# Down projections of two feed-forward blocks: sixteen of 22 chunks by seven products of quarters

## The chip, the cores and the metric

The kernel runs on one core of a Trainium2 chip. The metric is the device time of one execution in microseconds (us); the time before is 3135.24 us, the median of three runs (3134.79 to 3135.58). PE is TensorE's matmul row of the profile, PEld its weight loads, DVE is VectorE, ACT is ScalarE, POOL is GpSimd, SP is the engine whose queue issues nearly all DMAs.

## The reference, cut to what matters

Three blocks of a network run one after the other on 1024 tokens of width 1024. The first and the third end in a feed-forward part whose hidden width is D_FF = 2816, which is 22 chunks of 128. The change is in the last product of both, the down projection:

```
up = causal_depthwise_conv(h @ w_up[l], conv_w[l], conv_b[l])      # block 1
a, bgate = jnp.split(up, [D_FF], axis=-1)
x = x + (jax.nn.silu(a) * bgate) @ w_down[l]
```

Block 3 is the same without the conv, with x scaled by ALPHA, and with another norm behind it. All data are float32.

## The kernel before, in words

**Precision.** A float32 product is made of three matmuls. Each operand is split into hi, a copy in the reduced type F32R, and lo, the difference of the operand and hi. A product of 128 x 128 weights and 128 x 512 values is hi·hi + hi·lo + lo·hi (mm, line 345). split (line 349) makes hi on ScalarE and lo by a subtraction on GpSimd or VectorE.

**Layout.** Everything is transposed: features lie on partitions, tokens in two halves of 512 columns. X[j][half] holds feature block j (0 to 7) of the residual stream in SBUF. The gated hidden activations of chunk c and token half are written to DRAM (gd, g_out, line 173) and read back as G[c, half] (g_dma, line 1361). All weights stand in one DRAM array, wall, as tiles of 128 x 1024 in the order of their use, and SP loads them into raw.

**The up projections** (strassen, line 1256) already use seven products of quarters in place of eight. s_steps (line 1203) makes the weights' side of it out of two raw tiles ra and rb in six steps: A22, S1 and S3 are 512 wide, A1 and S24 are 1024 wide. Each is a cast on ScalarE and a subtraction on GpSimd, and four more GpSimd subtractions or additions form the sums. Raw tiles alternate between two pools (s_dma, line 1247).

**The down projections** (down, line 1423) take two chunks at a time: for each of 8 feature blocks and 2 halves one PSUM bank gets six matmuls, and VectorE adds it to X[j][half]. So each pair of chunks has 16 groups of six matmuls and 16 adds. Nine such pairs (18 chunks) are followed by the last four chunks, which are summed in PSUM over all four before a single add, since norms and outputs hang on them. Beside a pair, the next pair's G tiles are split: half 0 on GpSimd, half 1 on VectorE (g_split, line 1365). Weight tiles come through w_load (line 369), which keeps four of them split ahead; w_retire loads the next.

**Order.** The order of the program is fixed by hand: every engine carries out its instructions strictly in the order in which the Python code emits them, and waits at the head of its queue when an operand or a buffer is not there. self.bank gives PSUM banks from a pool of six, and pools hand out released buffers in the order of their release. The tag h has 64 buffers of 128 x 512 in SBUF. tail (line 1381) is called during the last round of the up projection: it starts the first weights, the first G tiles and the 16 X tiles (x_load, line 1376). In block 1 self.left then holds four pieces of the last chunk's conv, which down emits after its adds 0, 3, 6 and 9; in block 3 it holds one gate. Work of other generators (Driver, line 191) is not due in these stretches.

Of the kernel before, what the change touches and what calls it, by code (L numbers as in the profile page):

```python
# [9 lines left out]
F32 = mybir.dt.float32  # L10
# [29 lines left out]
def _weights(a):  # L40
# [9 lines left out]
    def ffn(up, down):  # L50
        ab = _chunks_a(a[up][0])
        dn = a[down][0].reshape(NFF, 128, D)
        out = []

        def u(c):
            out.extend([ab[c], ab[NFF + c]])

        for c in range(NFF):
            u(c)
        out.extend(dn[:NFF - 4])  # L60
        for j in range(4):
            out.append(np.concatenate([dn[k][:, 256 * j:256 * j + 256] for k in range(NFF - 4, NFF)], axis=1))
        return out

    t = []
# [32 lines left out]

S_TILES = ((38, 38), (178, 180))

# [198 lines left out]
class Kernel:  # L299
# [947 lines left out]
    def s_dma(self, n):  # L1247

        pool = self.up if (n + self.lead) % 2 else self.wp
        for _ in range(2):  # L1250
            raw = pool.tile([128, 1024], F32, tag="raw", bufs=2, name="raw")
            self.nc.sync.dma_start(out=raw, in_=self.a["wall"][self.wd])
            self.wd += 1
            self.sraws.append(raw)
# [77 lines left out]
    def ffn(self, evac, put, later, add_last, done, by_half, alpha=None, lead=2):  # L1332
# [5 lines left out]
        with ExitStack() as ctx:  # L1338
# [32 lines left out]

            def g_group(i):
                cs = (2 * i, 2 * i + 1) if i < NFF // 2 - 2 else range(NFF - 4, NFF)
                return [(c, half, i % 2 and c < NFF - 1) for c in cs for half in range(2)]

# [5 lines left out]
            def tail(n):  # L1381
# [6 lines left out]
                elif n == 1:  # L1388
                    for a in g_group(0):
                        g_dma(*a[:2])  # L1390
                    for j in range(2):
                        x_load(j)
                elif n == 2:
                    for j in range(2, 5):
                        x_load(j)
                else:
                    for a in g_group(0):
                        g_split(*a, nc.gpsimd)
                    for j in range(5, 8):
                        x_load(j)  # L1400
                    for a in g_group(1):
                        g_dma(*a[:2])

# [18 lines left out]

            def down(i, ws):
                n = 0
                loads = g_group(i + 1)
                gap = 12 // len(loads)
                for j in range(8):
                    for half in range(2):
                        ps = self.bank("dn")
                        for k in range(2):  # L1430
                            whi, wlo = ws[k]
                            ghi, glo = G[2 * i + k, half]
                            c = slice(128 * j, 128 * j + 128)
# [4 lines left out]
                        x = X[j][half]  # L1438
                        if alpha and i == 0:
                            self.stt(x, x, alpha, ps, ALU.mult, ALU.add)  # L1440
                        else:
                            self.tt(x, ps, x, ALU.add)
                        n += 1
                        if n % 3 == 1 and self.left:
                            self.left.pop(0)()
                        if n % gap == 0 and loads and n > 2:
                            g_split(*loads.pop(0))

            for i in range(NFF // 2 - 2):
                ws = self.w_take(2)  # L1450
                if i == 0:
                    self.w_retire(0)
                yield from down(i, ws)
                if i < NFF // 2 - 3:
                    for a in g_group(i + 2):
                        g_dma(*a[:2])
                self.w_retire(2)
            full, q0, q1 = slice(0, HF), slice(0, HF // 2), slice(HF // 2, HF)
# [1008 lines left out]
```

## Time and profile before

| | |
|---|---|
| median of the runs | 3135.24 us |
| profiled execution | 3131.53 us |
| span of the profiled execution | 3129.7 us |
| PE busy | 2941.2 us (94%) |
| DVE busy | 1803.3 us (58%) |
| POOL busy | 1432.9 us (46%) |
| ACT busy | 1284.8 us (41%) |
| mean granted clock | 0.964 |

The span is the time from the first to the last instruction. Matmuls are pipelined, so the duration of a single one (0.39 us) is longer than the distance to the next. Instructions of VectorE also overlap a little: the next one starts before the end shown for the one before. A row of the form "dn<-ghi,whi" names what is written and what is read; a wait stands in square brackets with what ended it. In the first block the down projection runs from about 904 to 1145 us, in the third from about 2851 to 3103.

### The profile page before, as it was taken

Reading aid. Unit: us, or ns where it says so; the run is one execution under the profiler, and the core shown is the slowest. Engines: PE = TensorE matmul, PEld = TensorE weight load, DVE = VectorE, ACT = ScalarE, POOL = GpSimd, SP = SyncE. Lnnn points to the kernel's source line nnn. Section 1 sums busy time; section 2 is a strip of 40 time slices with the busy share of each in tenths; the row PEclk is TensorE's granted clock in tenths of the full one; section 3 lists DMA queues with packets and bytes.
Section 4 is the critical chain, followed back from the end, with each engine's and each line's share of the span. In section 5 each row is a group of like instructions: output and inputs, shape, how many; then the busy total and the mean of one; then the engine's idle time right before and its main releaser. Section 6 shows DMA issues by size and latency. Waiting matters only on the chain. (4 is left out here: it accounts for less than half of the span.)

```text
span 3129.7 us, 41397 instructions
## 1 busy us (share of the span) xinstructions
PE 2941.2 (94%) x15188; PEld 2499.6 (80%) x15188; DVE 1803.3 (58%) x3522; ACT 1284.8 (41%) x2493; POOL 1432.9 (46%) x1008
## 2 busy tenths in 40 slices
PE   8999998999999999889998989989899899999997
PEld 6898776888878877868897778977678688888886
DVE  6444246666665569966645665577667522224556
ACT  4232224444432153556673356654444422222223
POOL 4313434777743365862214342144333477774330
PEclk9999999999999999999998989999889999999998
DMA  4101241222252312131113232110222222225321
GB/s 159 33 23 51 72 134 41 81 81 81 81 188 82 108 49 80 40 109 50 44 39 118 84 121 64 42 32 27 68 68 98 84 81 81 86 79 179 108 81 54
DMA packets 114876, 248.96 MB, mean 80 GB/s; under 512 B 19696, under 2 KB 31600, under 8 KB 114672
## 3 DMA queue, kind: packets, MB, share of 16 engines
q1 hardware_dynamic: 114384, 246.01, 24.0%
q8 instruction: 120, 1.97, 0.3%
q14 instruction: 84, 0.69, 0.1%
q10 hardware_dynamic: 288, 0.30, 0.0%
HBM read 192.52 MB, written 53.74 MB: 79 GB/s over the span
## 5 line engine op out<-in xcount | busy, mean ns | idle before, releaser
L332 POOL TENSOR_TENSOR wlo<-raw,whi 128x1024 fp32r<-128x1024 f32 x240 | 582.2, 2436 | 862.0 <-ACT whi L326 846.5
L326 ACT ACTIVATE whi<-raw 128x1024 fp32r<-128x1024 f32 x240 | 248.3, 1053 | 537.0 <-PE dn L347 283.2
L332 DVE TENSOR_TENSOR X<-dn,X 128x512 f32<-128x512 f32 (+1 forms) x312 | 209.9, 676 | 161.7 <-PE dn L347 159.5
L347 PE MATMUL dn<-ghi,whi 128*128 128x512 f32 (+1 forms) x736 | 281.1, 382 | 0.6 <-DVE X L332 0.6
L347 PE MATMUL dn<-glo,whi 128*128 128x512 f32 (+1 forms) x736 | 280.2, 381 | 0.0
L347 PE MATMUL dn<-ghi,wlo 128*128 128x512 f32 (+1 forms) x736 | 280.2, 381 | 0.0
L332 POOL TENSOR_TENSOR raw<-raw 128x512 f32<-128x512 f32 x156 | 203.0, 1302 | 12.1
L332 POOL TENSOR_TENSOR slo<-raw,shi 128x512 fp32r<-128x512 f32 x117 | 150.7, 1302 | 106.2 <-ACT shi L326 104.9
L347 PE MATMUL p<-thi,shi 128*128 128x512 f32 x468 | 185.1, 395 | 13.9 <-DVE u L1105 9.8
L332 DVE TENSOR_TENSOR v<-p,e 128x512 f32<-128x512 f32 x78 | 53.8, 690 | 243.8 <-ACT e L326 194.3
L347 PE MATMUL p<-tlo,shi 128*128 128x512 f32 x468 | 183.9, 393 | 0.0
L347 PE MATMUL p<-hhi,wlo 128*128 128x512 f32 x468 | 182.2, 389 | 1.7 <-POOL wlo L332 1.7
L347 PE MATMUL p<-thi,slo 128*128 128x512 f32 x468 | 183.7, 393 | 0.0
L347 PE MATMUL p<-hhi,whi 128*128 128x512 f32 x468 | 182.1, 389 | 0.0
L347 PE MATMUL p<-hlo,whi 128*128 128x512 f32 x468 | 182.1, 389 | 0.0
L329 DVE SCALAR_TENSOR_TENSOR t<-u,vec,t 128x512 f32<-128x512 f32 x176 | 132.9, 755 | 79.5 <-ACT t L326 74.2
L347 PE MATMUL qk<-hhi,whi 128*128 128x512 f32 x384 | 162.2, 422 | 7.8 <-ACT hhi L326 7.2
L332 POOL TENSOR_TENSOR beta<-beta,f 128x511 f32<-128x511 f32 (+3 forms) x96 | 91.2, 956 | 154.0 <-DVE beta L336 137.8
L347 PEld LDWEIGHTS dn<-ghi,whi 128*128 128x128 f32 x736 | 139.2, 189 | 27.6 <-DVE X L332 1.3
L347 PEld LDWEIGHTS dn<-ghi,wlo 128*128 128x128 f32 x736 | 139.1, 189 | 26.4
L347 PEld LDWEIGHTS dn<-glo,whi 128*128 128x128 f32 x736 | 139.2, 189 | 26.0
L347 PE MATMUL op<-hhi,wlo 128*128 128x512 f32 x384 | 153.2, 399 | 4.0 <-POOL wlo L332 4.0
(400 smaller groups left out, 8150.7 us busy)
## 6 DMA issues: line engine op xcount, KB each, us to landing
raw<-in_wall SPq DMA_DIRECT2D x240, 512.0 KB, 3.8
gd<-g SPq DMA_DIRECT2D x88, 256.0 KB, 2.2
gx<-gd SPq DMA_DIRECT2D x88, 256.0 KB, 5.2
x2d<-X SPq DMA_DIRECT2D x64, 256.0 KB, 2.0
X<-x2d SPq DMA_DIRECT2D x64, 256.0 KB, 5.3
x<-in_xT SPq DMA_DIRECT2D x16, 256.0 KB, 6.0
X<-in_xT SPq DMA_DIRECT2D x16, 256.0 KB, 4.6
T<-in_rpbx SPq DMA_DIRECT2D x8, 448.0 KB, 3.6
```

What stands on the lines that cost most here:

```text
L326: self.nc.scalar.activation(out=out, in_=in_, func=func, bias=bias, scale=scale, **kw)
L329: self.nc.vector.scalar_tensor_tensor(out=out, in0=in0, scalar=s, in1=in1, op0=op0, op1=op1)
L332: (eng or self.nc.vector).tensor_tensor(out=out, in0=in0, in1=in1, op=op)
L347: self.nc.tensor.matmul(out=out, lhsT=lhsT, rhs=rhs, start=start, stop=stop, skip_group_check=more)
```

## The change

In both blocks chunks 0 and 1 stay as they were (first_down). Chunks 2 to 17 become four quads of four chunks. Within a quad, the weights are a 2 x 2 arrangement of quarters (feature blocks 0 to 3 or 4 to 7, by the first or last two chunks of the quad), and so are the activations (first or last two chunks, by token half). Each quad is done in two sets, s = 0 and 1, of two feature blocks out of the upper and two out of the lower half. A set has seven products of two feature blocks each, so 14 groups of six matmuls; I number them 0 to 13, in the order of plan in seven(). There are no sums in SBUF of the products: a bank is accumulated further after it was read, and each state of it that belongs to some part of X is added there by VectorE, 14 adds a set. An even set is one with s = 0, an odd one has s = 1.

The weights' side comes out of s_steps as in the up projection, a set ahead. The activations' side, b_steps, is made on ScalarE and VectorE once per quad, for the next quad: products 1, 2 and 3 take G tiles as they are (two casts and two subtractions, "lows"), products 5, 6, 7 and 4 first form differences (two subtractions, two casts, two lows each). The differences of products 5, 6 and 4 are written to PSUM (t), those of product 7 over G in SBUF. todo says after which add of a set each step is emitted. The last four chunks are done as before; their splits are emitted during the last quad, and the weight loads through w_load stop in between (S_TILES). The conv pieces of block 1 are emitted after adds 0 to 3.

```diff
@@ -57,7 +57,10 @@
 
         for c in range(NFF):
             u(c)
-        out.extend(dn[:NFF - 4])
+        out.extend(dn[:2])
+        for i in range(2, NFF - 4, 4):
+            for col in (0, 512, 256, 768):
+                out.append(np.concatenate([dn[k][:, col:col + 256] for k in range(i, i + 4)], axis=1))
...
@@ -96,7 +99,7 @@

-S_TILES = ((38, 38), (178, 180))
+S_TILES = ((38, 38), (78, 78), (178, 180), (220, 220))
...
@@ -1246,7 +1249,9 @@
 
     def s_dma(self, n):
-        pool = self.up if (n + self.lead) % 2 else self.wp
+        self.s_raws(self.up if (n + self.lead) % 2 else self.wp)
+
+    def s_raws(self, pool):
         for _ in range(2):
             raw = pool.tile([128, 1024], F32, tag="raw", bufs=2, name="raw")
             self.nc.sync.dma_start(out=raw, in_=self.a["wall"][self.wd])
@@ -1369,9 +1374,13 @@
...
-            def g_group(i):
-                cs = (2 * i, 2 * i + 1) if i < NFF // 2 - 2 else range(NFF - 4, NFF)
-                return [(c, half, i % 2 and c < NFF - 1) for c in cs for half in range(2)]
+            def g_raw(cs):
+                for c in cs:
+                    for half in range(2):
+                        g_dma(c, half)
+
+            head, quads = (0, 1), [range(i, i + 4) for i in range(2, NFF - 4, 4)]
+            ends = range(NFF - 4, NFF)
 
...
@@ -1386,20 +1395,21 @@
                     self.w_load()
                     self.w_load()
                 elif n == 1:
-                    for a in g_group(0):
-                        g_dma(*a[:2])
+                    g_raw(head)
                     for j in range(2):
                         x_load(j)
+                    self.s_raws(self.up)
                 elif n == 2:
                     for j in range(2, 5):
                         x_load(j)
                 else:
-                    for a in g_group(0):
-                        g_split(*a, nc.gpsimd)
+                    for c in head:
+                        for half in range(2):
+                            g_split(c, half, False, nc.gpsimd)
                     for j in range(5, 8):
                         x_load(j)
-                    for a in g_group(1):
-                        g_dma(*a[:2])
+                    g_raw(quads[0])
+                    self.s_raws(self.wp)
 
...
-            def down(i, ws):
+            def b_steps(cs, B):
+
+                t = [None, None]
+
+                def pair(n, k, src):
+                    hi, lo = self.h("ghi", F32R), self.h("glo", F32R)
+                    B.setdefault(n, ([], []))
+                    B[n][0].append(hi)
+                    B[n][1].append(lo)
+                    self.act(hi, src, AF.Copy)
+                    return lo, src, hi
+
+                def raw(n, o, half):
+                    for low in [pair(n, k, G[cs[o + k], half]) for k in range(2)]:
+                        self.tt(*low, ALU.subtract)
+
+                def made(n, outs, parts):
+                    lows = []
+                    for k in range(2):
+                        p, q = parts(k)
+                        self.tt(outs(k), p, q, ALU.subtract)
+                        lows.append(pair(n, k, outs(k)))
+                    for low in lows:
+                        self.tt(*low, ALU.subtract)
+
+                def t1():
+                    for k in range(2):
+                        t[k] = self.pt.tile([128, 512], F32, tag="t", name="t")
+                    made(5, lambda k: t[k], lambda k: (G[cs[k], 1], G[cs[k], 0]))
+
+                return [lambda: raw(1, 0, 0), t1,
+                        lambda: made(6, lambda k: t[k], lambda k: (G[cs[2 + k], 1], t[k])),
+                        lambda: raw(2, 2, 0),
+                        lambda: made(7, lambda k: G[cs[k], 1], lambda k: (G[cs[2 + k], 1], G[cs[k], 1])),
+                        lambda: raw(3, 2, 1),
+                        lambda: made(4, lambda k: t[k], lambda k: (G[cs[2 + k], 0], t[k]))]
+
+            def first_down(ws, todo):
                 n = 0
-                loads = g_group(i + 1)
-                gap = 12 // len(loads)
                 for j in range(8):
                     for half in range(2):
                         ps = self.bank("dn")
                         for k in range(2):
                             whi, wlo = ws[k]
-                            ghi, glo = G[2 * i + k, half]
+                            ghi, glo = G[k, half]
                             c = slice(128 * j, 128 * j + 128)
                             self.mm(ps, whi[:, c], ghi, k == 0, False)
                             self.mm(ps, whi[:, c], glo, False, False)
                             self.mm(ps, wlo[:, c], ghi, False, k == 1)
                         yield 6 * 216.0
                         x = X[j][half]
-                        if alpha and i == 0:
+                        if alpha:
                             self.stt(x, x, alpha, ps, ALU.mult, ALU.add)
                         else:
                             self.tt(x, ps, x, ALU.add)
+                        if self.left:
+                            self.left.pop(0)()
+                        for f in todo.get(n, ()):
+                            f()
                         n += 1
-                        if n % 3 == 1 and self.left:
-                            self.left.pop(0)()
-                        if n % gap == 0 and loads and n > 2:
-                            g_split(*loads.pop(0))
-
-            for i in range(NFF // 2 - 2):
-                ws = self.w_take(2)
-                if i == 0:
-                    self.w_retire(0)
-                yield from down(i, ws)
-                if i < NFF // 2 - 3:
-                    for a in g_group(i + 2):
-                        g_dma(*a[:2])
-                self.w_retire(2)
+
+            def seven(s, A, B, todo):
+
+                banks, n = {}, 0
+                plan = ((1, "c", "A1", 0, 0, 0), (5, "f", "S1", 0, 4, 1), (6, "c", "S24", 0, 0, 1),
+                        (2, "d", "A1", 512, 0, 0), (7, "c", "S3", 0, 4, 1), (3, "f", "S24", 512, 0, 1),
+                        (4, "c", "A22", 0, 4, 0))
+                for p, key, w, off, row, half in plan:
+                    for m in range(2):
+                        start = (key, m) not in banks
+                        if start:
+                            banks[key, m] = self.bank("dn")
+                        ps = banks[key, m]
+                        whi, wlo = A[w]
+                        for k in range(2):
+                            c = slice(off + 256 * k + 128 * m, off + 256 * k + 128 * m + 128)
+                            hi, lo = B[p][0][k], B[p][1][k]
+                            self.mm(ps, whi[:, c], hi, start and k == 0, False, not start)
+                            self.mm(ps, whi[:, c], lo, False, False, not start)
+                            self.mm(ps, wlo[:, c], hi, False, k == 1, not start)
+                        yield 6 * 216.0
+                        x = X[row + 2 * s + m][half]
+                        self.tt(x, ps, x, ALU.add)
+                        for f in todo.get(n, ()):
+                            f()
+                        n += 1
+
+            A, B = {}, {}
+            ss, bs = self.s_steps(0, A), b_steps(quads[0], B)
+            todo = {2 * i: [f] for i, f in enumerate(ss)}
+            for n, f in zip((5, 7, 9, 11, 13, 15), bs):
+                todo.setdefault(n, []).append(f)
+            ws = self.w_take(2)
+            yield from first_down(ws, todo)
+            self.w_retire(2)
+            over = bs[6:]
+            n_sets = 2 * len(quads)
+            for n in range(n_sets):
+                i, s = n // 2, n % 2
+                todo = {1: over} if n == 0 else {}
+
+                def at(x, f):
+                    todo.setdefault(x, []).append(f)
+
+                nxt = {}
+                if n + 2 < n_sets:
+                    self.s_raws(self.wp if n % 2 else self.up)
+                if n + 1 < n_sets:
+                    for x, f in zip((0, 1, 2, 5, 7, 10), self.s_steps(n + 1, nxt)):
+                        at(x, f)
+                if s == 0:
+                    nb, cs = {}, quads[i + 1] if i + 1 < len(quads) else ends
+                    at(2, lambda cs=cs: g_raw(cs))
+                    if i + 1 < len(quads):
+                        bs = b_steps(cs, nb)
+                        for x, f in zip((8, 10, 12), bs):
+                            at(x, f)
+                    else:
+                        for x, c in zip((6, 8, 10, 12), cs):
+                            at(x, lambda c=c: g_split(c, 0, False))
+                elif i + 1 < len(quads):
+                    for x, f in zip((3, 5, 7, 9), bs[3:]):
+                        at(x, f)
+                else:
+                    def more():
+                        del self.stops[0]
+                        self.wi += 2 * n_sets
+                        self.w_load()
+                        self.w_load()
+
+                    at(0, more)
+                    for x, c in zip((3, 5, 7, 9), ends):
+                        at(x, lambda c=c: g_split(c, 1, c < NFF - 1))
+                yield from seven(s, A, B, todo)
+                A = nxt
+                if s:
+                    B = nb
+            self.w_retire(0)
...
```

## Rows read from the trace of the kernel before

**Rows 1.** The page, busy time, share of the span and instructions

```profile
PE 2941.2 (94%) x15188; PEld 2499.6 (80%) x15188; DVE 1803.3 (58%) x3522; ACT 1284.8 (41%) x2493; POOL 1432.9 (46%) x1008
```

**Rows 2.** Stretches of the span, with their columns, both projections

```profile
core 0: us, PE busy (x) PEld busy (x) DVE busy (x) ACT busy (x) POOL busy (x), PEclk, DMA share, GB/s
560.00:880.00 320.00, 320.00 (x1414) 265.05 (x1412) 202.88 (x354) 147.53 (x218) 229.49 (x150) 1.00 0.24 80
926.00:948.00 22.00, 22.00 (x98) 18.00 (x97) 15.36 (x24) 4.60 (x7) 7.80 (x4) 1.00 0.47 156
2850.00:3050.00 200.00, 200.00 (x885) 165.58 (x884) 113.42 (x167) 42.19 (x62) 73.62 (x42) 1.00 0.37 123
```

**Rows 3.** Instructions in order of time (start, us), around one slot

```profile
1000.27 0.39 PE L347 MATMUL dn<-ghi,whi 128*128 128x512 f32 x1
1000.47 0.69 DVE L332 TENSOR_TENSOR X<-dn,X 128x512 f32<-128x512 f32 x1 [0.67 <-PE dn L347]
1001.07 0.68 DVE L332 TENSOR_TENSOR glo<-gx,ghi 128x512 fp32r<-128x512 f32 x1
1001.63 0.39 PE L347 MATMUL dn<-ghi,whi 128*128 128x512 f32 x1
```

**Rows 4.** Groups by line and shape: count, busy us, mean ns, idle before

```profile
L332 POOL TENSOR_TENSOR wlo<-raw,whi 128x1024 fp32r<-128x1024 f32 x240 | 582.2, 2436 | 862.0 <-ACT whi L326 846.5 <-issue 15.1 <-DVE ql L329 0.5
L332 DVE TENSOR_TENSOR X<-dn,X 128x512 f32<-128x512 f32 x296 | 203.3, 690 | 161.1 <-PE dn L347 158.9
L332 POOL TENSOR_TENSOR raw<-raw 128x512 f32<-128x512 f32 x156 | 203.0, 1302 | 12.1
L332 DVE TENSOR_TENSOR glo<-gx,ghi 128x512 fp32r<-128x512 f32 x40 | 28.3, 708 | 3.7 <-ACT ghi L326 3.7
```

**Rows 5.** In order of time, ScalarE and GpSimd before the first projection

```profile
887.44 1.06 ACT L326 ACTIVATE whi<-raw 128x1024 fp32r<-128x1024 f32 x1 [9.28 <-DMA raw<-in_wall]
888.58 4.72 POOL L332 TENSOR_TENSOR wlo<-raw,whi 128x1024 fp32r<-128x1024 f32 x2 [9.87 <-ACT whi L326]
899.37 2.19 ACT L326 ACTIVATE ghi<-gx 128x512 fp32r<-128x512 f32 x4
```

**Rows 6.** In order of time, VectorE and GpSimd around 520

```profile
519.33 2.40 POOL L332 TENSOR_TENSOR wlo<-raw,whi 128x1024 fp32r<-128x1024 f32 x1 [13.66 <-ACT whi L326]
520.56 3.42 DVE L332 TENSOR_TENSOR X<-X 128x512 f32<-128x512 f32 x2
521.80 3.32 POOL L332 TENSOR_TENSOR raw<-raw 128x512 f32<-128x512 f32 x2
526.29 2.39 POOL L332 TENSOR_TENSOR wlo<-raw,whi 128x1024 fp32r<-128x1024 f32 x1 [1.17 <-ACT whi L326]
527.74 1.49 DVE L332 TENSOR_TENSOR tlo<-X,thi 128x512 fp32r<-128x512 f32 x1 [3.76 <-ACT thi L326]
```

**Rows 7.** Groups by line and shape, block 2's convolution

```profile
L329 DVE SCALAR_TENSOR_TENSOR cd<-u,vec,cd 128x512 f32<-128x512 f32 x133 | 100.2, 754 | 3.6
L332 POOL TENSOR_TENSOR cp<-cp,cm 128x512 f32<-128x512 f32 x70 | 91.3, 1307 | 34.5 <-ACT cm L326 30.3
```

**Rows 8.** In order of time, VectorE on a piece of conv

```profile
919.48 1.55 DVE L329 SCALAR_TENSOR_TENSOR t<-u,vec,t 128x512 f32<-128x512 f32 x2
921.06 0.69 DVE L332 TENSOR_TENSOR g<-t,a 128x512 f32<-128x512 f32 x1
```

**Rows 9.** The stretch in which the last projection begins

```profile
2850.00:2870.00 20.00, 20.00 (x90) 16.55 (x89) 11.48 (x18) 5.35 (x8) 10.04 (x7) 1.00 1.02 385
```

**Rows 10.** Stretches after the first projection, and TensorE's wait in them

```profile
1150.00:1155.00 5.00, 2.28 (x14) 2.20 (x14) 3.56 (x4) 4.49 (x7) 3.78 (x3) 0.85 0.00 2
1155.00:1160.00 5.00, 5.00 (x14) 4.03 (x15) 2.96 (x4) 3.34 (x5) 5.00 (x4) 0.50 0.18 29
1160.00:1165.00 5.00, 5.00 (x31) 4.36 (x30) 3.11 (x15) 0.21 (x2) 1.29 (x5) 0.96 0.21 80
1152.54 1.05 PE L347 MATMUL st<-ones,s 128*128 128x1 f32 x8 [3.87 <-POOL s L332]
```

## The prediction

> **What bounds the kernel now.** I read the page's busy shares first, then cut the span into stretches around the two down projections, then opened one product group, and last looked at each engine's queue around it. On the page TensorE is busy 94% of the span [rows 1]. In the stretches it is busy for all 22.00 us of 926 to 948 and for all 200.00 us of 2850 to 3050, at full clock, while VectorE works 113, GpSimd 74 and ScalarE 42 of those 200 us [rows 2]: the down projections are TensorE's alone. One group of six matmuls takes 1000.27 to 1001.63, so 1.36 us, 0.2267 us a matmul [rows 3]. I call such a group a slot. VectorE's add of a slot into X begins 0.20 us after the slot, and an instruction queued behind it starts 0.60 us later [rows 3], though the add itself lasts 0.69 [rows 4].
>
> **The change, part by part.**
>
> *Matmuls.* Sixteen chunks cost 8 pairs x 16 slots = 128 slots per block now, and 8 sets x 14 = 112 afterwards. 16 slots x 1.36 = 21.8 us go per block, 43.5 us in all, as long as nothing else keeps TensorE waiting.
>
> *Work on the other engines.* X adds fall from 128 to 112 per block. Per quad of chunks (two sets, 38.1 us of TensorE) VectorE gets 28 adds and 22 subtractions: 50 x 0.605 = 30.3 us. GpSimd gets per set seven 512-wide and two 1024-wide subtractions: at 1.27 and 2.38 us apart [rows 4, 5] 13.7 us, so 27.3 per quad; the up projections already run it 229 of 320 us beside a fully busy TensorE [rows 2]. ScalarE has 14 + 6 casts at about 0.56 and 4 at 1.0 [rows 5], 15 us. By busy time alone everything fits, and the full 43.5 us would be won. What decides is how the queues hold one another.
>
> *How late an add may be.* Banks are handed out in the order of their release, so a new set does not wait for the last adds of the old one. But plan's key "c" accumulates products 1, 6, 7 and 4 in the same two banks with an add between each: slot 4 needs add 0, slot 8 add 4, slot 12 add 8, with three slots (4.08 us) between. VectorE may thus lag about 3.1 us. In the kernel before no add sat behind more than one or two other instructions, and a bank came up again only after five further slots.
>
> *The port.* At 519.33 GpSimd starts a 2.40 us subtraction; VectorE's X<-X pair begins at 520.56 and takes 3.42 us instead of about 1.3 (0.605 and 0.69). Read through: the first of the pair gets on only when GpSimd's ends at 521.73, GpSimd's next (two in 3.32 instead of 2 x 1.30 [rows 4]) then goes, and the second waits for it. At 527.74 a tlo takes 1.49 instead of 0.69: it ends 0.55 after GpSimd's instruction [rows 6]. So VectorE and GpSimd alternate, one instruction each; a delayed VectorE instruction costs 0.47 after the other has ended, and GpSimd gets on about 0.45 after that starts. Where one VectorE operand is in PSUM there is nothing of it: the conv's 133 steps on cd average 754 ns, beside GpSimd's 70 at 1307 [rows 7]. The new subtractions with both inputs in SBUF are the lows of products 1, 2 and 3, the differences of product 5 and all four of product 7: 12 of 22 per quad, beside a GpSimd that is busy 72% of the time.
>
> The Trainium skill (SBUF — State Buffer, Who interferes with whom) says that a VectorE instruction with two SBUF inputs contends with a GpSimd instruction that reads SBUF, and that whoever starts first holds the pair for the whole instruction; it speaks against this change. The rows agree on the exclusion, but GpSimd gets on after 0.45 us of a 0.69 us instruction; with the whole time between instructions held, the walk below loses 6 to 7 us more.
>
> *One quad, step by step* (us from the start of an even set; casts and lows reach the next engine 0.08 after their shown end, as wlo at 888.58 follows the cast that ended at 888.50 [rows 5]). GpSimd's last subtraction of the set before ends at 3.2, its next five end at 4.4, 5.7, 7.0, 8.3, 9.5, then the 1024-wide one at 11.9. Adds 0 to 8 are on time, add 8 until 13.05. Product 1's lows: 13.2 to 13.6, then GpSimd until 14.9, then until 15.4. Adds 9 and 10 until 16.6. Product 5's differences meet GpSimd's S24 subtraction (16.1 to 18.5); that product is through at 21.1, adds 11 and 12 at 22.3, product 6 at 24.95, add 13 at 25.55. The set's matmuls ended at 19.04. Odd set: add 0 ends at 26.2, slot 4 was due at 24.48 and starts at 26.3: **1.84 lost**. ScalarE was held by product 6's casts until 24.2, so GpSimd's new round starts at 24.9 and its S3 subtraction ends only at 31.25; product 2's casts stand behind S3's cast (29.4), the first low waits for cast and port until 31.25, the second for the 1024-wide one until 34.1. Add 4, ready at 27.9, ends at 35.2; slot 8 was due at 31.77 and starts at 35.3: **3.56 lost**. Product 7 runs 35.8 to 39.5, adds 6 and 7, product 3 until 41.9, add 8 until 42.5; slot 12, due at 40.77, starts at 42.7: **1.94 lost**. Product 4 follows and the next even set starts with VectorE 0.4 us behind, as at first. A quad so takes 45.4 us; the same four chunks now take 32 slots, 43.5.
>
> *Whole down projection.* Quads 1 and 2 lose 7.34 each. Quad 3 has no next quad to prepare: 0. Quad 0 loses 12.0, since 18 of its own subtractions begin in first_down's slot 5 and VectorE enters set 0 behind (add 0 is through 9 us late, slot 4 starts 5.7 late). Block 3: 26.7 us. Block 1 has also four conv pieces, now in first_down's slots 0 to 3 rather than 0, 3, 6 and 9, each some 1.5 us of steps and up to 0.69 for the gate [rows 8]; first_down's VectorE work is then about 16 x 0.605 + 18 x 0.605 + 9 = 30 us against 21.8 of slots, which costs 7 more beyond what six banks cushion: 33.6. Together 60.3 lost against 43.5 won: **16.8 us slower**.
>
> *Other edits.* The tail's burst carries 1 MB more before first_down (8 G loads instead of 4; the weight loads are as many as before) at a time when the DMA engines are full (385 GB/s [rows 9]): at most 3 us per block; G is needed from slot 5 on and the second pair of raws a phase later, so I take 0. On SP's queue block 1's two gd writes now stand behind 10 issues instead of 4; they are read in set 6. The half-0 splits of the last chunks move 5 us of GpSimd work to set 6, when nothing on VectorE contends.
>
> *Clock.* A wait of 3.87 us was followed by granted 0.85, 0.50 and 0.96 in three 5 us stretches (0.50 is the 1.2 GHz level) [rows 10]: 3.4 us of matmul time. Eight waits here come near or beyond that. Since the next wait behind each would take up what is lost, I take 0, and up to 1.5 for each of the six 3.56 us waits and 3.4 for each of the two 5.7 us ones, 16 us, as the upper end.
>
> *Sum.* The profiled execution took 3131.53 us (span 3129.7 and 1.8 around it); with 16.8 more it is 3148.3. The median of the runs is 3.7 above that execution: **3152 us**.
>
> **The rivals.** *The port hardly decides (faster).* If VectorE's subtractions fall mostly into GpSimd's gaps, the same walk without port waits loses 2.3 us in block 3 (quad 0: 0.6; 0.9 at set 1's slot 12; 0.4 in quads 1 and 2 each) and 9.2 in block 1 (first_down 3.1, set 0 4.5, the rest 1.6): 3135.2 - 43.5 + 11.5 = 3103 us. For it: glo<-gx,ghi now averages 708 ns on VectorE, nearly undelayed [rows 4]. Against it: GpSimd is then busy 37% [rows 2], not 72%. *Half of the port waits.* The order of two queues turns on tenths of a us: if the 1024-wide subtraction does not cut in (2.4 us of the 3.56), and the differences of product 5 miss S24's, a quad loses 3 to 4, quad 0 7, block 1 some 6 more: about 38 to 40 lost, 3131 us. It is here that the sign turns. *Clock and burst on top.* All the upper ends at once: 3152 + 16 + 6 = 3174; against it, slow matmuls give VectorE time to catch up.
>
> **How the numbers follow.** Forecast 0.53, its own range 3139 to 3166 (one 1024-wide wait more or less per quad, 6 x 2.4 us); hardly any port loss 0.24, 3100 to 3125; half 0.15, 3126 to 3139; clock and burst 0.08. Runs within 0.2% (6.3 us) of 3135 count as the same. Faster: 0.24 + 0.05 of the half case and 0.01 of the forecast, 0.30. Same: 0.09 of the half case and 0.06 of the forecast, 0.15. Slower: 0.55. The range reaches from inside the first rival to inside the last: 3106 to 3169.
>
> **What would show it.** Right: TensorE in 948 to 1060 and 2890 to 3010 is no longer full, with waits for VectorE's X adds at slots 4, 8 and 12 of odd sets, 1.5 to 4 us each; low and difference subtractions on VectorE average over 0.9 us with single ones over 2; the last quad runs without waits. Wrong: some 174 us per block up to the last four chunks (196 now) with TensorE full, subtractions near 0.69 us, or waits on weights (S24, A1) or on B operands in place of the adds.

## The result, and the profile after

The changed kernel took 3151.28 us (median of 5 runs, 3144.81 to 3153.57) against 3134.79 (5 runs, 3131.87 to 3135.58): 1.0055 times as long, with a 95% interval of 1.0044 to 1.0065. That is 16.5 us slower; 16.8 were forecast, and single runs of the changed kernel lie up to 8.8 us apart. The profiled execution took 3149.68 us, its span is 3147.9 and its mean granted clock 0.958.

The page's busy line, the stretches of [rows 2], and for [rows 9] the 20 us before and the first 20 us of block 3's projection, which starts at 2861.4 here and at 2851.7 before (the columns are those of [rows 2]):

```profile
PE 2918.7 (93%) x14996; PEld 2472.8 (79%) x14996; DVE 1909.3 (61%) x3634; ACT 1341.7 (43%) x2589; POOL 1541.4 (49%) x1088
```

```profile
926.00:948.00 22.00, 14.25 (x54) 10.48 (x53) 21.52 (x30) 9.58 (x17) 7.48 (x5) 0.92 0.36 120
2850.00:3050.00 200.00, 180.34 (x750) 145.14 (x749) 159.52 (x211) 68.24 (x107) 127.16 (x82) 0.95 0.37 124
...
2841.00:2861.00 20.00, 20.00 (x90) 16.55 (x89) 5.12 (x8) 5.92 (x9) 8.37 (x5) 1.00 0.96 347
2861.00:2881.00 20.00, 20.00 (x90) 16.57 (x89) 15.88 (x20) 5.98 (x10) 13.44 (x10) 1.00 0.70 257
```

TensorE is no longer full: it stands for 7.8 of 22 us in one stretch and for 19.7 of 200 in the other, and its clock is no longer 1.00. VectorE now works 160 of the 200 us, where it worked 113. Around the start of block 3's projection (2841 to 2881) TensorE stays full under 257 to 347 GB/s: the larger burst of loads cost nothing there.

Every wait of TensorE of 0.25 us or more in block 3's projection, in order of time (start, us, the instruction, and in brackets the wait before it with its releaser):

```profile
2887.15 0.47 PE L350 MATMUL dn<-ghi,shi 128*128 128x512 f32 x1 [0.86 <-DVE X L332]
2895.39 0.77 PE L350 MATMUL dn<-ghi,whi 128*128 128x512 f32 x1 [5.24 <-DVE X L335]
2917.28 0.47 PE L350 MATMUL dn<-ghi,whi 128*128 128x512 f32 x1 [0.53 <-DVE X L335]
2926.31 0.50 PE L350 MATMUL dn<-ghi,shi 128*128 128x512 f32 x1 [3.31 <-DVE X L335]
2962.71 0.47 PE L350 MATMUL dn<-ghi,whi 128*128 128x512 f32 x1 [1.56 <-DVE X L335]
2971.64 0.79 PE L350 MATMUL dn<-ghi,shi 128*128 128x512 f32 x1 [3.23 <-DVE X L335]
3007.97 0.47 PE L350 MATMUL dn<-ghi,whi 128*128 128x512 f32 x1 [1.50 <-DVE X L335]
3016.97 0.79 PE L350 MATMUL dn<-ghi,shi 128*128 128x512 f32 x1 [3.31 <-DVE X L335]
```

All of them wait for an add into X, none for weights. A matmul with shi is on S1, S3 or A22, one with whi on A1 or S24; counted from the projection's first matmul, the 0.86 stands at slot 2 of set 0 (S1), the 5.24 at slot 4 of set 0 (S24), the 0.53 and the 1.5s at slot 4 and the 3.3s at slot 8 (S3) of odd sets, the places that the walk named. At slot 12 of the odd sets, which it named too, block 3 has none. After 3017 there is none either.

VectorE's groups of 948 to 1075, by line and shape (count, busy us, mean ns, idle before):

```profile
L335 DVE TENSOR_TENSOR X<-dn,X 128x512 f32<-128x512 f32 x78 | 50.0, 682 | 11.2 <-PE dn L350 11.2
L335 DVE TENSOR_TENSOR glo<-gx,ghi 128x512 fp32r<-128x512 f32 x24 | 28.5, 1215 | 6.8 <-ACT ghi L329 6.8
L335 DVE TENSOR_TENSOR glo<-t,ghi 128x512 fp32r<-128x512 f32 x16 | 10.4, 687 | 0.7
L335 DVE TENSOR_TENSOR t<-gx 128x512 f32<-128x512 f32 x6 | 8.6, 1472 | 0.0
L335 DVE TENSOR_TENSOR t<-gx,t 128x512 f32<-128x512 f32 x12 | 7.7, 686 | 0.0
L335 DVE TENSOR_TENSOR gx<-gx 128x512 f32<-128x512 f32 x6 | 7.1, 1222 | 0.0
```

The same operation on the same shape: where an input is a PSUM tile (dn, t) it takes 682 to 687 ns, where both are in SBUF (gx) 1215 to 1472. Before, glo<-gx,ghi averaged 708 [rows 4].

One such pair (product 2's lows), as VectorE's and then GpSimd's queue have it (start, us):

```profile
2961.28 3.07 DVE L335 TENSOR_TENSOR X<-dn,X 128x512 f32<-128x512 f32 x5
2966.40 4.58 DVE L335 TENSOR_TENSOR glo<-gx,ghi 128x512 fp32r<-128x512 f32 x2 [2.04 <-ACT ghi L329]
2970.91 1.27 DVE L335 TENSOR_TENSOR X<-dn,X 128x512 f32<-128x512 f32 x2
```

```profile
2965.14 2.55 POOL L335 TENSOR_TENSOR slo<-raw,shi 128x512 fp32r<-128x512 f32 x2
2967.91 2.52 POOL L335 TENSOR_TENSOR wlo<-raw,whi 128x1024 fp32r<-128x1024 f32 x1 [0.23 <-ACT whi L329]
```

Product 2's two lows take 4.58 us in place of 1.29. The first ends at 2968.23, 0.55 after GpSimd's second 512-wide subtraction (2967.68); the 1024-wide one starts between the two, and the second low ends at 2970.98, 0.55 after that (2970.43). The add behind ends at 2971.58, and TensorE goes on at 2971.64 after standing 3.23: the step that the prediction walked through.

### The profile page after: what moved, and what is told of

Same layout as the page of the kernel before. It is cut to its first block, busy times and chain, and to the rows that moved or that the text cites. A ratio compares the mean times of both kernels' runs of the same rounds, so it can differ in the third digit from the quotient of the medians.

```text
span 3147.9 us, 41208 instructions
## 1 busy us (share of the span) xinstructions
PE 2918.7 (93%) x14996; PEld 2472.8 (79%) x14996; DVE 1909.3 (61%) x3634; ACT 1341.7 (43%) x2589; POOL 1541.4 (49%) x1088
## 5 line engine op out<-in xcount | busy, mean ns | idle before, releaser
L335 POOL TENSOR_TENSOR raw<-raw 128x512 f32<-128x512 f32 x220 | 293.7, 1335 | 16.9
L335 POOL TENSOR_TENSOR slo<-raw,shi 128x512 fp32r<-128x512 f32 x165 | 212.4, 1301 | 165.6 <-ACT shi L329 164.3
L335 DVE TENSOR_TENSOR X<-dn,X 128x512 f32<-128x512 f32 (+1 forms) x280 | 179.2, 668 | 66.1 <-PE dn L350 65.8
L350 PE MATMUL dn<-ghi,whi 128*128 128x512 f32 (+1 forms) x480 | 184.5, 384 | 21.5 <-DVE X L335 20.6
L329 ACT ACTIVATE shi<-raw 128x512 fp32r<-128x512 f32 x165 | 103.0, 627 | 196.1 <-POOL raw L335 186.1
L350 PE MATMUL dn<-glo,whi 128*128 128x512 f32 (+1 forms) x480 | 182.1, 379 | 0.0
L350 PE MATMUL dn<-ghi,wlo 128*128 128x512 f32 (+1 forms) x480 | 182.1, 379 | 0.0
L350 PE MATMUL qk<-hlo,whi 128*128 128x512 f32 x384 | 156.1, 407 | 1.4 <-DVE hlo L332 1.4
L350 PE MATMUL qk<-hhi,wlo 128*128 128x512 f32 x384 | 156.1, 406 | 0.0
```

The lines of the kernel that those rows point to most:

```text
L329: self.nc.scalar.activation(out=out, in_=in_, func=func, bias=bias, scale=scale, **kw)
L335: (eng or self.nc.vector).tensor_tensor(out=out, in0=in0, in1=in1, op=op)
L350: self.nc.tensor.matmul(out=out, lhsT=lhsT, rhs=rhs, start=start, stop=stop, skip_group_check=more)
```

## The experiments

Each changes the kernel after the change and is compared with the kernel before on the same chip. That took 3133.63 us beside the first four and 3132.92 beside the last two. "Lost" is the time from a projection's first matmul to the first of its last four chunks, less the 174.1 us that its 128 slots take of a full TensorE, in the profiled execution; the kernel after the change lost 34.6 us in block 1 and 30.5 in block 3.

**1. Inputs from PSUM.** Products 2, 3 and 7 read the PSUM tile t in place of one SBUF input (so these three products are formed from other numbers); count, order and engine of all instructions stay.

```diff
-                    for low in [pair(n, k, G[cs[o + k], half]) for k in range(2)]:
-                        self.tt(*low, ALU.subtract)
+                    for k, (lo, src, hi) in enumerate([pair(n, k, G[cs[o + k], half]) for k in range(2)]):
+                        self.tt(lo, src if n == 1 else t[k], hi, ALU.subtract)
...
-                    for low in lows:
-                        self.tt(*low, ALU.subtract)
+                    for k, (lo, src, hi) in enumerate(lows):
+                        self.tt(lo, t[k] if n == 7 else src, hi, ALU.subtract)
...
-                        lambda: made(7, lambda k: G[cs[k], 1], lambda k: (G[cs[2 + k], 1], G[cs[k], 1])),
+                        lambda: made(7, lambda k: G[cs[k], 1], lambda k: (t[k], G[cs[k], 1])),
```

> Changes part of the computation: the subtractions of products 2, 3 and 7 read the PSUM tile t in place of one of their SBUF inputs (8 of the 12 subtractions per quad with two SBUF inputs); number, size and order of all instructions stay. Port theory: the queue walk with these eight free of GpSimd loses 10 us in block 3 and 17 in block 1 instead of 27 and 34, so 33 us less than the changed kernel's 3151: about 3118; the waits of 3.3 us at slot 8 of odd sets nearly vanish (0.3), those of about 1.5 at slot 4 stay. Rival (VectorE has too many instructions in its queue, whichever memory they read): no change, 3151.

Measured: 3119.8 us (3111.63 to 3121.06), 0.9949 times before, with a 95% interval of 0.9936 to 0.9962 (below, such intervals stand in square brackets). It lost 18.4 us in block 1 and 13.1 in block 3, for 17 and 10 expected. VectorE's and GpSimd's queues at the like place of block 1 (start, us):

```profile
1006.55 1.29 DVE L335 TENSOR_TENSOR glo<-t,ghi 128x512 fp32r<-128x512 f32 x2 [2.11 <-ACT ghi L329]
1007.75 1.28 DVE L335 TENSOR_TENSOR X<-dn,X 128x512 f32<-128x512 f32 x2
1008.95 1.28 DVE L335 TENSOR_TENSOR gx<-t,gx 128x512 f32<-128x512 f32 x2
```

```profile
1005.28 2.57 POOL L335 TENSOR_TENSOR slo<-raw,shi 128x512 fp32r<-128x512 f32 x2
1008.07 2.40 POOL L335 TENSOR_TENSOR wlo<-raw,whi 128x1024 fp32r<-128x1024 f32 x1 [0.21 <-ACT whi L329]
```

The two lows run beside GpSimd in 1.29 us. At slot 8 TensorE has no wait of 0.25 us or more left; in this odd set it waits at slot 4 and, for 0.5 us, at slot 12:

```profile
1002.79 0.47 PE L350 MATMUL dn<-ghi,whi 128*128 128x512 f32 x1 [1.45 <-DVE X L335]
1014.72 0.50 PE L350 MATMUL dn<-ghi,shi 128*128 128x512 f32 x1 [0.49 <-DVE X L335]
```

So the second SBUF input is what costs, not the number of instructions in the queue. The wait at slot 4 stays, as expected with products 1 and 5 left as they are.

**2. The lows of products 1, 2 and 3 on GpSimd**, where they stand in the queue of its own subtractions.

```diff
-                        self.tt(*low, ALU.subtract)
+                        self.tt(*low, ALU.subtract, nc.gpsimd)
```

> The six lows per quad of products 1, 2 and 3 run on GpSimd instead of VectorE. Port theory: VectorE loses six instructions and half of its conflicts, GpSimd rises from 27 to 35 of 38 us per quad; the walk loses 6 us in block 3 and 12 in block 1, 42 less than now: about 3109, faster than the kernel before. Rival (GpSimd becomes the bound, weights of the next set arrive late): waits on S24, A1 or product 1 to 3 at about 1 to 3 us per set, 3135 or slower.

Measured: 3118.93 us (3108.38 to 3122.15), 0.9947 [0.9933, 0.9962]. No wait on weights, though GpSimd works 82 of 92 us (948 to 1040), so the rival is out. Ten us of the gain are missing. In part they are in the projections: these lost 16.7 us in block 1 and 12.6 in block 3, where the walk had 12 and 6. The largest waits stand at slot 4 of sets 0 and 1 (3.86 and 2.35 in block 3), and the granted clock was 0.84 in 926 to 948. Another part lies outside: between the two projections, where the code is the same, this profiled execution took 1756.7 us and that of the kernel after the change 1747.2.

**3. Product 2's step two slots earlier.**

```diff
-                    for x, f in zip((3, 5, 7, 9), bs[3:]):
+                    for x, f in zip((1, 5, 7, 9), bs[3:]):
```

> Product 2's casts and lows are emitted after add 1 of an odd set instead of add 3, so that its casts stand ahead of those of S1 and S3 on ScalarE. Order theory (the casts behind S3's cast are the cause): the six 3.3 us waits at slot 8 go, 20 us less: 3131. Port theory with the walk: the wait at slot 8 goes, but product 7's four subtractions then meet the 1024-wide one and the wait at slot 12 grows from 1.6 to about 4.9; 4 us less in all: 3147.

Measured: 3154.5 us (3150.97 to 3161.24), 1.0069 [1.0056, 1.0083]. The waits at slot 8 are gone, and slot 12 has longer ones in their place:

```profile
967.32 0.47 PE L350 MATMUL dn<-ghi,whi 128*128 128x512 f32 x1 [1.53 <-DVE X L335]
982.96 0.80 PE L350 MATMUL dn<-ghi,shi 128*128 128x512 f32 x1 [4.48 <-DVE X L335]
1014.00 0.47 PE L350 MATMUL dn<-ghi,whi 128*128 128x512 f32 x1 [0.73 <-DVE X L335]
1029.67 0.57 PE L350 MATMUL dn<-ghi,shi 128*128 128x512 f32 x1 [4.50 <-DVE X L335]
```

The walk had 4.9 there. The order theory (3131 us) is out, and the walk's 3147 was 7 short. Behind each of the two long ones the clock was lower (0.66 in 980 to 990, 0.83 in 1030 to 1040). The two projections lost 66.9 us together, 1.8 more than in the kernel after the change, where the walk had 4 less: matmuls at the lower clock cost some 2 us more, but the waits did not shrink either. Moving one step alone moves the wait.

**4. A fresh bank for every product** (the accumulation of products over one another is left out), so that no slot waits for an add three slots before.

```diff
-                        start = (key, m) not in banks
-                        if start:
-                            banks[key, m] = self.bank("dn")
-                        ps = banks[key, m]
+                        start = True
+                        ps = self.bank("dn")
```

> Leaves out the accumulation over products: each of the 14 groups of a set takes a fresh bank, so a bank comes up again after five further slots (6.8 us) instead of three (4.1). If the chain of product sums in one bank were what makes late adds costly, most of the loss in the sets goes: 45 us lost in the sets shrinks to under 15, about 3120. By the walk VectorE's and GpSimd's queues stay as long, the cushion is used up once and then the waits return at slots 10 and 12: 46 us lost instead of 60, 14 less: 3137.

Measured: 3142.07 us (3128.18 to 3145.04, 11 runs), 1.0021 [1.001, 1.0032]. The waits behind set 0 now come when all six banks wait for adds, at slots 10 and 12 of odd sets (and, of 0.5 us, at slot 2 of even ones):

```profile
969.95 0.50 PE L350 MATMUL dn<-ghi,whi 128*128 128x512 f32 x1 [2.52 <-DVE X L335]
974.90 0.62 PE L350 MATMUL dn<-ghi,shi 128*128 128x512 f32 x1 [1.92 <-DVE X L335]
```

Together they are 4.4 us in this quad, where the kernel after the change had 1.54 and 3.28: the chain of two banks sets where a late add is felt, but only about 10 us of the loss (the projections lost 28.6 and 23.7 us, 12.7 less together; the walk had 14 less).

**5. and 6. Other slots.** With the queues walked as in the prediction I searched for slots at which no add is late. Number 6 has these slots with all subtractions of the activations on VectorE; number 5 also gives the lows of products 1 and 3 to GpSimd.

```diff
-                        if self.left:
+                        if self.left and (n in (0, 1, 6, 7) or n > 7):
...
-            todo = {2 * i: [f] for i, f in enumerate(ss)}
-            for n, f in zip((5, 7, 9, 11, 13, 15), bs):
+            todo = {}
+            for n, f in zip((0, 1, 5, 6, 7, 10), ss):
+                todo.setdefault(n, []).append(f)
+            for n, f in zip((7, 8, 10, 11, 11, 15), (bs[1], bs[0], bs[2], bs[3], bs[4], bs[5])):
...
-                    for x, f in zip((0, 1, 2, 5, 7, 10), self.s_steps(n + 1, nxt)):
+                    for x, f in zip((0, 5, 6, 7, 10, 12) if s else (0, 1, 6, 7, 7, 10), self.s_steps(n + 1, nxt)):
...
-                        for x, f in zip((8, 10, 12), bs):
+                        for x, f in zip((9, 9, 10), bs):
...
-                    for x, f in zip((3, 5, 7, 9), bs[3:]):
+                    for x, f in zip((3, 9, 10, 11), (bs[4], bs[6], bs[3], bs[5])):
```

and in number 5 besides

```diff
-                        self.tt(*low, ALU.subtract)
+                        self.tt(*low, ALU.subtract, nc.vector if n == 2 else nc.gpsimd)
```

> Theory (queue order on VectorE, with the port's alternation, sets the loss): the same work, moved to slots at which the queue walk finds no add late (weight steps of even sets at slots 0, 1, 6, 7, 7, 10 and of odd sets at 0, 5, 6, 7, 10, 12; products 1, 5, 6 at 9, 9, 10 of the even set, 7, 4, 2, 3 at 3, 9, 10, 11 of the odd one; first_down re-timed too), and the lows of products 1 and 3 on GpSimd. The walk loses 4.8 us in block 1 and 0 in block 3, against 33.6 and 26.7 in the changed kernel: 3151 - 55.5 = 3096 us; with the 10 us by which the kernel with lows on GpSimd missed its walk, 3106. No wait of TensorE over 1 us in either down projection, and the granted clock stays full there. Rival (a floor that the walk doesn't have, from GpSimd's 72% share and the clock): waits only move to other slots, as when product 2 was moved alone, and the time stays near 3119, that of the kernel with lows on GpSimd.

> Same slots as the re-timed kernel, but all subtractions of B stay on VectorE. Theory (order and port): the walk loses 11.1 us in block 1 (3.1 of it at slot 4 of set 0) and 6.3 in block 3, so 3151 - 42.9 = 3108 us; the 3.3 us waits at slot 8 of odd sets are gone without any change of engine. Rival (VectorE's load is what counts, wherever its steps stand): it stays within 10 us of the changed kernel, 3141 to 3151.

Measured: number 5 took **3089.05 us** (3087.57 to 3089.6), 0.9864 [0.9851, 0.9878]; number 6 took 3106.77 (3103.75 to 3111.79), 0.9926 [0.9912, 0.994]. Stretches of number 5, and all its waits of 0.25 us or more in both projections:

```profile
926.00:948.00 22.00, 19.21 (x84) 15.29 (x83) 20.26 (x32) 9.85 (x17) 17.85 (x14) 1.00 0.41 144
948.00:1040.00 92.00, 92.00 (x408) 76.17 (x407) 76.53 (x116) 36.16 (x58) 80.45 (x54) 1.00 0.35 113
2870.00:3030.00 160.00, 160.00 (x721) 132.99 (x719) 119.04 (x174) 53.14 (x82) 117.26 (x75) 1.00 0.26 83
```

```profile
922.56 0.50 PE L350 MATMUL dn<-ghi,whi 128*128 128x512 f32 x1 [0.88 <-DVE X L335]
931.37 0.50 PE L350 MATMUL dn<-ghi,shi 128*128 128x512 f32 x1 [2.79 <-DVE X L335]
2855.45 0.50 PE L350 MATMUL dn<-ghi,shi 128*128 128x512 f32 x1 [0.85 <-DVE X L332]
```

TensorE is full and at full clock but for slot 14 of first_down and slot 2 of set 0 in block 1, and slot 2 of set 0 in block 3 (4.5 us of waits in all, against 44.6 in the kernel after the change). It lost 4.5 us in block 1 and 1.1 in block 3, for 4.8 and 0 walked; one wait of 2.79 is over the 1 us expected. The gain over the kernel before, 3132.92 - 3089.05 = 43.9 us, is about what the removed matmuls are worth (43.5), but not all of it is theirs: in the profiled executions the projections up to the last four chunks became 39.0 us shorter (392.9 to 353.9), and 3.6 us lie where the code is the same. The time came out 7 better than the 3096 expected. That figure took the walk's 60.3 off 3151 as what the changed kernel loses, and it really lost 65.1 (below); and on the chip on which the 3151 were measured the kernel before took 2 us more than on this one.

In number 6 every instruction runs on the engine that it had in the kernel after the change, so the slots alone are worth some 40 us (ratios to before of 1.0055 and 0.9926). It lost 11.0 us in block 1 and 8.6 in block 3, for 11.1 and 6.3 walked. The lows on GpSimd give the last 18, at the starts of the projections above all: waits of 2.81 and 1.59 at slots 2 and 4 of set 0 in block 1, of 2.05 and 2.86 in block 3, remain in number 6. The port still holds part of its subtractions. The differences of products 5 and 7 now average 0.69 and 0.68 us in 948 to 1075, but the lows with two SBUF inputs still more than 1 us there, for 1215 ns in the kernel after the change:

```profile
L335 DVE TENSOR_TENSOR glo<-gx,ghi 128x512 fp32r<-128x512 f32 x24 | 23.8, 1034 | 0.5 <-ACT ghi L329 0.5
```

Single ones take up to 2886 ns. Reckoned over both projections, VectorE's subtractions with two SBUF inputs took 54 us more than 0.69 each in the kernel after the change and 24 more in number 6. The slots thus took away more than half of the delay at the port, and what is left stands where TensorE seldom waits for the adds behind it.

## Why the prediction was right

**The won 43.5 us** are there: 192 fewer matmuls stand on the page (14996 for 15188 [rows 1]), and number 5, which loses 4.5 us more than the kernel before in its two projections, has them 39.0 us shorter.

**The lost 60.3 us.** The 128 slots of a projection are 174.1 us of full TensorE. In block 1 they last from 905.5 to 1114.2, so 34.6 are lost (33.6 predicted), in block 3 from 2861.4 to 3066.0, 30.5 (26.7). Together that is 65.1, 4.8 more than predicted. The kernel before lost 1.1 there itself, so the two projections, up to their last four chunks, became 20.4 us longer (392.9 to 413.3), but the span only 18.2: the time before the first projection grew by 1.7 us, and the stretch between the two, whose code is the same, took 3.6 less (1747.2 for 1750.8). Over the eight profiled executions of this document that stretch took 1747.2 to 1756.7. So the walk was good to some 5 of 60 us, and that the forecast met the median within 1 us is in part luck.

**A quad.** From slot 4 of one odd set to the same of the next it is 2962.71 - 2917.28 = 45.43, then 45.26, and in block 1 44.99 (966.65 to 1011.64) and 45.33 (to 1056.97): 45.4 was predicted. The single waits, predicted and measured: slot 4 of set 0, 5.7 and 5.2; slot 4 of odd sets 1.84 and 1.5 in four of six, 0.5 and 0.4 in the others; slot 8, 3.56 and 3.3; slot 12, 1.94 and 1.6 in the one of six where it appears. Quad 3 has none, as said. A steady quad came out right within 0.4 us, though not wait by wait. The mis-sized term is block 3's entry: without quads 1 and 2 (45.43 + 45.26 less 2 x 38.08, so 14.5) it lost 16.0 for 12.0. Behind the 5.24 us wait the clock was 0.53 in 2895 to 2900, which cost some 2.2 us of matmul time, and the next wait, 0.53, took up next to nothing of it (the prediction's 12.0 leaves 0.8 for that wait, less 5.7, 3.56 and 1.94); the 0.86 us at 2887 were not predicted either.

**The port** was read rightly off [rows 6]: single subtractions with two SBUF inputs went up to 2892 ns (mean 1215), and experiment 1 shows that the second SBUF input makes the difference. The first rival (port hardly decides, 3103 us) is out for this order of the queues. Number 6, with the same engines in another order, comes near its time (3106.77 us), and by its mechanism only in part: the port's delay is 24 us there in place of 54, not near nothing, and TensorE mostly does not wait for what is left. "Half of the port waits" did not come either.

**The clock**, taken as 0 with 16 us as its upper end, is where the sum was right by a balance that only half was argued. Ten-us stretches of after in which it fell:

```profile
945.00:955.00 10.00, 10.00 (x41) 8.11 (x40) 8.29 (x13) 4.22 (x7) 7.48 (x5) 0.89 0.06 5
...
975.00:985.00 10.00, 9.35 (x29) 7.50 (x30) 9.72 (x15) 3.09 (x6) 2.84 (x2) 0.68 0.18 54
1065.00:1075.00 10.00, 9.03 (x31) 6.98 (x32) 9.85 (x15) 2.76 (x5) 3.17 (x2) 0.83 0.37 112
2890.00:2900.00 10.00, 4.76 (x13) 3.70 (x12) 9.94 (x14) 4.55 (x9) 6.12 (x5) 0.66 0.43 153
2920.00:2930.00 10.00, 6.69 (x24) 5.07 (x23) 8.78 (x8) 3.90 (x7) 8.21 (x5) 0.85 0.15 53
2970.00:2980.00 10.00, 8.24 (x28) 6.36 (x29) 9.84 (x14) 2.31 (x4) 3.76 (x3) 0.83 0.17 52
3010.00:3020.00 10.00, 6.69 (x24) 5.14 (x23) 8.28 (x7) 3.37 (x6) 8.86 (x6) 0.79 0.16 54
3020.00:3030.00 10.00, 10.00 (x40) 8.06 (x40) 9.72 (x17) 4.22 (x7) 2.24 (x1) 0.87 0.49 157
```

What is missing to 1.00, times 10 us, with three more stretches at 0.94, 0.98 and 0.98, makes some 17 us. In a part of that time TensorE stood anyway; the matmuls that did run at the lower clock cost 13.9 us more than at the full one. TensorE's idle times in the 21 waits of 0.25 us or more are 25.1 and 19.5, together 44.6; from start to start of the matmuls, as the walk counts, they are 48.0, some 12 less than the 60.3 predicted. The 3.2 us that are left of the 65.1 are smaller pauses. The prediction said that the next wait behind a slow stretch would take up what is lost there, and that can be seen: in quad 1 of block 1, where the clock stayed at 1.00 after the 3.34 of slot 8, slot 12 waits 1.61; in block 3, after the 3.23 at 2971.64, the granted clock is 0.57 in 2971 to 2975, and slot 12 has no wait of 0.25 us or more. The quads are equally long (45.33 and 45.26). VectorE sets the pace, and TensorE may wait or run slowly. Behind the 5.24 of quad 0 in block 3 no wait took it up, and the clock cost extra. So the clock's term was not 0: some 14 us stood in place of some 12 us of waits, and what it added beyond them was small.

**The other edits** at 0: TensorE has no wait on the weights of a set, and none that leads back to G or gd is to be seen. Of waits on an activation operand, which would have spoken against the walk, the profile has one: 0.89 us on ghi at the start of set 0 in block 1 (932.45). It is hardly the operand's: the slot takes the bank of first_down's slot 10, whose add began at 931.62, and in the three waits before it, at slots 10, 12 and 14, TensorE went on 0.73 to 0.74 us after such an add began. By that it would have started at 932.36 without the operand, so some 0.1 us is the operand's. ScalarE waited once for a G tile, 0.40 us at 2991.4, and TensorE's waits in that quad are no longer than in the others.

## What to carry to other kernels

Here, cutting the bounding engine's work put the helpers' queue order in charge. In such a case walk the queues with the durations of the trace, add by add, before the change, and let that walk choose the slots. Here the same instructions in other slots are some 40 us apart, and with four of the 14 lows of a quad on GpSimd besides, a loss of 16 us becomes a gain of 44. Look first for instructions with two SBUF inputs on VectorE beside a busy GpSimd: a PSUM input (number 1) or GpSimd itself (numbers 2 and 5) takes them out of the alternation, and other slots (number 6) shorten the delay and put what is left where no add is due soon.

## What the runs showed of the hardware

Of the kernel after, TensorE's six waits of 3.2 to 3.3 us at slot 8 were followed by a lower granted clock in five cases (0.50 in 975 to 980, 0.50 in 3016 to 3020, 0.66 in 2926 to 2931) and by 1.00 in one (1020.67), though all stand at the same slot behind the same work. Of five waits of 2.79 to 2.93 us in numbers 1, 5 and 6 four were followed by 0.58 to 0.75 and the 2.79 of number 5 by 1.00; the waits of 4.37 us and more in the projections of the kernel after and of number 3 were all followed by 0.50 to 0.72. Even the same wait of 1.91 us, at slot 10 of first_down in block 1, was followed by 1.00 in the kernel after (in 921 to 925) and by 0.66 in number 2 (in 919 to 923); first the kernel after, then number 2:

```profile
921.19 0.50 PE L350 MATMUL dn<-ghi,whi 128*128 128x512 f32 x1 [1.91 <-DVE X L335]
918.83 0.50 PE L350 MATMUL dn<-ghi,whi 128*128 128x512 f32 x1 [1.91 <-DVE X L335]
```

At the lower level (1.2 GHz) matmuls of 512 columns came 0.43 us apart in place of 0.227. What tells equal waits apart stays open.

GpSimd can be run very full: with three products' lows on it, it worked 82 of 92 us, and TensorE had no wait on its results. Its 512-wide subtraction keeps its 1.30 us beside a VectorE whose subtractions have one PSUM input (number 1: 2.57 for two at 1005.28); the kernel after's raw<-raw, beside subtractions with two SBUF inputs, took 1.60 and 1.73 at 2970.51 and 2972.19.

The Trainium skill (SBUF — State Buffer, Who interferes with whom) says that a VectorE instruction with at most one SBUF input, outside the perf modes that use both port pairs, does not contend with GpSimd. Experiment 1 agrees: its 96 lows that read t have a median of 686 ns and a longest of 693, beside a GpSimd busy 60 of 92 us (948 to 1040).
